# A hybrid decoder trunk on one core: the leftovers of an expert dispatch, the transposes of `hs` and the row additions change places

## The chip, the core and the metric

The kernel runs on one core of one Trainium2 chip as a single program. A core has five instruction queues that work side by side and wait for one another only through semaphores: TensorE (PE; its weight loads are shown apart as PEld), VectorE (DVE), ScalarE (ACT), GpSimd (POOL) and SyncE (SP), which here only issues transfers. The metric is device time in microseconds (us), the median of several runs.

## The reference, cut to what matters

The reference is a decoder trunk of two layers over 256 tokens of width 1024. Each layer mixes tokens (layer 0: an RG-LRU group beside sparse attention; layer 1: a gated short convolution), cross-attends into 256 memory tokens, and then applies a mixture of 16 experts. A final RMS norm closes it. The change touches only the mixture, which both layers run:

```
gate = top-2 experts of the top-1 group, softmax weights        # (256, 16), two nonzeros a row
for e in range(16):
    h = silu(xt @ w_gate[e]) * (xt @ w_up[e])                   # (256, 512)
    y = y + gate[:, e:e+1] * (h @ w_down[e])                    # (256, 1024)
h = h + y
```

## The kernel before, in words

**Dispatch.** Each expert gets at most 64 tokens (`CAP`), so two experts make a pair of 128 rows, and a layer has eight pairs, 0 to 7. `dispatch` builds a 0/1 matrix `Pm` (L561) and multiplies the tokens with it (`gB`, L578, 32 products), which gives the pair's gathered tokens `XgT`, copied out by DVE and ACT in turn (L586, L588). What is left of a dispatch is its inner function `rest`, handed back as `last_part`. For pairs 0 to 5 (`by_rows`) it is two tiny products (`ptC`, L597) and some six small DVE operations (L601 to L608), which give each row its gate weight `gsl` and its destination `row`. For pairs 6 and 7 it transposes `PG`, made on POOL (L564), into `ptC` (L616) and copies that into `PT` (L618, L619).

**A pair.** `expert_pair` is a generator in four pieces, divided by `yield`: the first half of the gate products (`egA`, 16 of the 32 on L714); the second half; the 32 up products (`euA`, also L714) and the activation that makes `hs` (L724 to L726); four transposes of `hs` into `hC` (L731) and the copy `hT` (L733). After those come the 32 down products (`eyA`, `eyO`, L738) and the way back. Pairs 0 to 5 scale the result to `y` and scatter it by an indirect transfer from POOL into the DRAM buffers `yd` (L747). Pairs 6 and 7 split the scaled result into `yh` (ACT, L756) and `yl` (DVE, L757), multiply both with `PT` (`poB`, L761, L762) and add that to the residual `h` on DVE (L215).

**The order.** The loop at the end of `moe` lays the pieces of the next pair between those of the current one: next pair's dispatch, first gate half of the next, transposes of the current, second gate half of the next, down products of the current, up products of the next. Pair 4 (`BREAK`) is the exception: its dispatch stands before a branch for overflowing experts, and the program is divided there into blocks. Inside a block a planner sets every engine's queue when the program is built. It takes, by its own estimates of when inputs, weights and tiles are there, the ready instruction that was written earliest, so that an instruction written later can stand ahead of one that it takes to be waiting. On the chip each queue then keeps that order, ready or not. `first()` raises the priority of what is written inside it. Tiles with the tag `s2` (`Pm`, `PG`, `hs`, `hT`, `yh`, `yl`) share three buffers.

**Rows back.** What the pairs 0 to 5 scattered is read back by `add_rows`, called where the last pair, 7, is dispatched: eight transfers from POOL bring `yd` into two tiles `yr` (L830), and four DVE additions put them on `h` (L833).

**Weights.** SP streams them through a ring of twenty 1 MB places (L672) in the order gate of pair n, down of pair n-1, up of pair n. A place is free once TensorE has used it.

Of the kernel before, what the change touches and what calls it, by code (L numbers as in the profile page):

```python
# [19 lines left out]
D = 1024  # L20
T = 256
TT = 2
# [3 lines left out]
NE = 16  # L26
# [6 lines left out]
BREAK = 4  # L33
# [26 lines left out]
def hybrid_trunk_kernel(ctx: ExitStack, tc: tile.TileContext, x, mem, positions, norm_mix, norm_xattn,  # L60
# [6 lines left out]
    V, S, P, G = nc.vector, nc.scalar, nc.tensor, nc.gpsimd  # L67
# [13 lines left out]
    def bank(tag, name="ps"):  # L81
        return psum[tag].tile([128, 512], F32, tag=tag, name=name + tag)
# [10 lines left out]
    def x8(shape, name, dt=F32):  # L93
        return extra.tile(shape, dt, tag="x", name=name)

    def first(n=4000):
        return tc.high_priority(offset=n)
# [6 lines left out]
    h = const.tile([128, TT, D], F32, name="h")  # L104
# [6 lines left out]
    ident = const.tile([128, 128], F32, name="ident")  # L111
# [100 lines left out]
    def h_add(tt, half, ps, ss=None):  # L212

        hs = h[:, tt, half * 512:(half + 1) * 512]
        V.tensor_add(hs, hs, ps)  # L215
        if ss is not None:
            square_sum(hs, ss[:, half, tt:tt + 1], "S")

    def new_ss():
        ss = sm.tile([128, 2, TT], F32, name="ss2")  # L220
        ss_of_h.append(ss)
        return ss
# [127 lines left out]
    def run(gen, n=10 ** 6):  # L350
        for _ in range(n):
            if next(gen, 0) == 0:
                return
# [290 lines left out]
    def chunks_ahead(l):  # L644

        down = []
        for n in range(NE // 2):
            gate, up, next_down = pair_chunks(l, 2 * n, 4, DOWN_LAST if n == NE // 2 - 1 else DOWN)
            yield from down + gate + up if n == BREAK else gate + down + up
            down = next_down  # L650
        yield from down
# [46 lines left out]
        def used(self, n):  # L698
            pass

    def expert_pair(mp, l, stream, pair, step, cuts, by_rows, ss=None, rest=None):


        XgT = pair[0]
        acc = {}
        for nm in "gu":
            acc[nm] = bank("A", "e" + nm)
            for j0 in range(0, J, step):
                with first() if rest else nullcontext():
                    ws = stream.take(2)  # L710
                    for jj in range(step):
                        j = j0 + jj
                        for i in range(2):
                            P.matmul(acc[nm][i * 64:(i + 1) * 64, :], XgT[:, j, i * 64:(i + 1) * 64], ws[i][jj],  # L714
                                     start=(j == 0), stop=(j == J - 1))
                    stream.used(2)
                    if rest:
                        rest()
                        rest = None
                if nm == "g" and j0 + step in (J // 2, J):  # L720
                    yield
        PT, gsl = pair[1:]
        hs = mp.tile([128, DE], F32, name="hs", tag="s2", bufs=3)
        S.activation(hs, acc["g"], AF.Tanh, scale=0.5)  # L724
        V.scalar_tensor_tensor(hs, hs, 1.0, acc["g"], op0=ALU.add, op1=ALU.mult)  # L725
        V.scalar_tensor_tensor(hs, hs, 0.5, acc["u"], op0=ALU.mult, op1=ALU.mult)  # L726
        yield
        hp = bank("C", "h").rearrange("p (j s) -> p j s", j=4)
        h4 = hs.rearrange("p (f j) -> p f j", j=4)
        for j in range(4):  # L730
            P.transpose(hp[:, j, :], h4[:, :, j], ident)  # L731
        hT = mp.tile([128, 4, 128], F32, name="hT", tag="s2", bufs=3)
        S.copy(hT, hp)  # L733
        yield
        py = [bank("A", "ey"), bank("O", "ey")]

        def down(nh, j, i, w):
            P.matmul(py[nh][i * 64:(i + 1) * 64, :], hT[:, j, i * 64:(i + 1) * 64], w,  # L738
                     start=(j == 0), stop=(j == 3))

        def back_by_rows(nh):
            y = mp.tile([128, 512], F32, name="y", bufs=2)
            if nh:
                V.tensor_scalar(y, py[nh], gsl, None, op0=ALU.mult)
            else:
                S.activation(y, py[nh], AF.Copy, scale=gsl)  # L746
            G.indirect_dma_start(out=Yd[l][nh], out_offset=bass.IndirectOffsetOnAxis(ap=PT[:, 0:1], axis=0), in_=y,  # L747
                                 in_offset=None, bounds_check=2 * T - 1, oob_is_err=False)

        def back(nh):  # L750
            if by_rows:
                return back_by_rows(nh)

            yh, yl = (mp.tile([128, 512], F32R, name=nm, tag="s2", bufs=3) if ss is None else
                      spl.tile([128, 512], F32R, name=nm, tag=t) for nm, t in (("yh", "hi"), ("yl", "lo")))
            S.activation(yh, py[nh], AF.Copy, scale=gsl)  # L756
            V.scalar_tensor_tensor(yl, py[nh], gsl, yh.bitcast(F32), op0=ALU.mult, op1=ALU.subtract)  # L757
            for tt in range(TT):
                po = bank("B", "po")
                ts_ = slice(tt * 128, (tt + 1) * 128)  # L760
                P.matmul(po, PT[:, ts_], yh, start=True, stop=False)  # L761
                P.matmul(po, PT[:, ts_], yl, start=False, stop=True)  # L762
                h_add(tt, nh, po, ss)

        for c0, cn, j0, jn in cuts:
            ws = stream.take(2)
            halves = range(c0 // 512, (c0 + cn) // 512)
            for jj in range(jn):
                for nh in halves:
                    for i in range(2):  # L770
                        down(nh, j0 + jj, i, ws[i][jj][:, nh * 512 - c0:nh * 512 - c0 + 512])
            stream.used(2)
            if j0 + jn == 4:
                for nh in halves:
                    back(nh)

    def moe(l, ring, fill=None, n_fill=0):
        with ExitStack() as mctx:
            mp = mctx.enter_context(tc.tile_pool(name=f"moe{l}", bufs=1, reuse_waits="tile"))
            if fill is not None:  # L780
                run(fill, n_fill)
            stream = Stream(chunks_ahead(l), ring)
# [30 lines left out]
            def overflow():  # L813
                n_over = nc.values_load(over[0:1, 0:1])
                with tc.If(n_over > 0):  # L815
                    with tc.For_i(0, 3, 1):
                        V.tensor_scalar(posm2, posm2, float(-CAP), None, op0=ALU.add)
                        rest = Direct(chunks_in_turn(l), mp)
                        for e in range(0, NE, 2):
                            pairs, last_part = dispatch(mp, l, xs, gate, vals, posm2, e, 2, True, "XgO")  # L820
                            last_part()
                            run(expert_pair(mp, l, rest, pairs[0], 1, DOWN_ROWS, True))

            def add_rows():

                for r in range(2):
                    yr = x8([128, TT, D], "yr")
                    for tt in range(TT):
                        for nh in range(2):
                            nc.gpsimd.dma_start(yr[:, tt, nh * 512:(nh + 1) * 512],  # L830
                                                Yd[l][nh][r * T + tt * 128:r * T + (tt + 1) * 128, :])
                    for tt in range(TT):
                        V.tensor_add(h[:, tt, :], h[:, tt, :], yr[:, tt, :])  # L833

            def experts():

                for n in range(NE // 2):
                    with first() if n == 0 else nullcontext():
                        (pair,), last_part = dispatch(mp, l, xs, gate, vals, posm, 2 * n, 2, n < ROWS_PAIRS)
                        if n:  # L840
                            last_part()
                    last = n == NE // 2 - 1
                    if last:
                        add_rows()
                    yield expert_pair(mp, l, stream, pair, 4, DOWN_LAST if last else DOWN, n < ROWS_PAIRS,
                                      new_ss() if last else None, None if n else last_part)

            pairs = experts()
            cur = next(pairs)
            run(cur, 3)  # L850
            for n in range(1, NE // 2):
                if n == BREAK:
                    nxt = next(pairs)
                    run(cur)
                    overflow()
                    cur = nxt
                    run(cur, 3)
                    continue
                nxt = next(pairs)
                run(nxt, 1)  # L860
                run(cur, 1)
                run(nxt, 1)
                run(cur)
                run(nxt, 1)
                cur = nxt
            run(cur)

# [463 lines left out]
```

## Time and profile before

| what | value |
|---|---|
| runs shown | 972.27 us median of 3 (966.81 to 973.39) |
| the profiled execution | 972.64 us, its span 970.8 us |
| PE, PEld busy | 911.2 us (94%), 592.3 us (61%) |
| DVE, ACT, POOL busy | 395.9, 326.1, 85.2 us |
| mean granted TensorE clock | 0.970 of full speed |
| L714, gate and up products, both layers | 1024 products, 124.0 and 124.9 us busy |
| mixture of layer 0, of layer 1 | from about 278 to 508 us, from about 732 to 962 us of the span |

Times in the rows are microseconds from the start of the span. In a timeline row the first number is the start, the second the duration, `xN` the number of merged instructions, and the bracket the idle time of the engine before the row with what ended it. In the granted clock 1.00 is 2.4 GHz and 0.50 is 1.2 GHz.

### The profile page before, as it was taken

Reading aid. Unit: us, or ns where it says so; the run is one execution under the profiler, and the core shown is the slowest. Engines: PE = TensorE matmul, PEld = TensorE weight load, DVE = VectorE, ACT = ScalarE, POOL = GpSimd, SP = SyncE. Lnnn points to the kernel's source line nnn. Section 1 sums busy time; section 2 is a strip of 40 time slices with the busy share of each in tenths; the row PEclk is TensorE's granted clock in tenths of the full one; section 3 lists DMA queues with packets and bytes.
Section 4 is the critical chain, followed back from the end, with each engine's and each line's share of the span. In section 5 each row is a group of like instructions: output and inputs, shape, how many; then the busy total and the mean of one; then the engine's idle time right before and its main releaser. Section 6 shows DMA issues by size and latency. Waiting matters only on the chain.

```text
span 970.8 us, 13231 instructions
## 1 busy us (share of the span) xinstructions
PE 911.2 (94%) x5197; PEld 592.3 (61%) x5197; DVE 395.9 (41%) x830; ACT 326.1 (34%) x605; POOL 85.2 (9%) x144
## 2 busy tenths in 40 slices
PE   7999999999989997999889999999999999899875
PEld 5898678898754333433338998998875333333321
DVE  6846776645441111111327665644453221111132
ACT  5546575645321111111128444645431111110012
POOL 1000160000020100011100000000011000000201
PEclk9999999999999998999999999999999999999988
DMA  7955166568869999999993555557885999999981
GB/s 256 305 178 115 44 203 189 173 235 322 312 248 422 417 420 413 420 419 420 399 342 118 187 175 179 181 201 294 320 316 233 421 417 421 414 421 417 418 333 43
DMA packets 83023, 285.45 MB, mean 294 GB/s; under 512 B 15112, under 2 KB 16224, under 8 KB 62468
## 3 DMA queue, kind: packets, MB, share of 16 engines
q1 hardware_dynamic: 78468, 272.82, 74.6%
q0 software_dynamic: 4480, 11.65, 3.3%
q8 instruction: 45, 0.74, 0.3%
q14 instruction: 30, 0.25, 0.1%
HBM read 275.94 MB, written 11.53 MB: 296 GB/s over the span
## 4 chain that ended last, share of the span: by engine, by line
PE 34%; issue 14%; DMA 8%; DVE 2%; ACT 1%; POOL 1%; POOLq 0%; ACTq 0%; DVEq 0%
DMA yd<-y,row 5%; PE euA L714 4%; PE FA L316 4%; PE FA L321 4%; PE FA L319 4%; DMA yr<-yd 3%; PE egA L714 3%; PE TA L295 2%; PE TA L296 2%; PE TA L297 2%; PE eyA L738 2%; PE eyO L738 2%; PE gB L578 1%; PE sB L408 1%; PE poB L762 1%
## 5 line engine op out<-in xcount | busy, mean ns | idle before, releaser
L275 DVE TENSOR_TENSOR lo<-w,hi 128x1024 fp32r<-128x1024 f32 x122 | 147.7, 1222 | 124.8 <-ACT hi L274 85.4
L274 ACT CAST hi<-w 128x1024 fp32r<-128x1024 f32 x122 | 125.9, 1047 | 89.0 <-PE FA L321 48.7
L714 PE MATMUL egA<-we,XgT 128*64 128x512 f32 x512 | 124.0, 614 | 8.9 <-DVEq L815 6.4
L714 PE MATMUL euA<-we,XgT 128*64 128x512 f32 x512 | 124.9, 615 | 0.0
L714 PEld LDWEIGHTS egA<-we,XgT 128*64 128x64 f32 x512 | 40.9, 141 | 74.6 <-issue 65.0
L714 PEld LDWEIGHTS euA<-we,XgT 128*64 128x64 f32 x512 | 41.9, 141 | 70.5 <-issue 65.5
L738 PE MATMUL eyA<-we,hT 128*64 128x512 f32 x256 | 70.2, 597 | 3.0 <-ACT hT L733 3.0
L738 PE MATMUL eyO<-we,hT 128*64 128x512 f32 x256 | 72.2, 594 | 0.0
L319 PE MATMUL FA<-xh,hi 128*128 128x256 f32 x272 | 70.4, 292 | 1.9 <-ACT xh L250 1.8
L321 PE MATMUL FA<-xl,hi 128*128 128x256 f32 x272 | 70.0, 290 | 1.8 <-DVE xl L251 1.8
L586 ACT ACTIVATE XgT<-gB,ffn 128x128 f32<-128x128 f32 x64 | 22.5, 367 | 113.8 <-DVE XgT L588 113.8
L319 PEld LDWEIGHTS FA<-xh,hi 128*128 128x128 f32 x272 | 53.2, 196 | 3.8 <-ACT xh L250 2.5
L321 PEld LDWEIGHTS FA<-xl,hi 128*128 128x128 f32 x272 | 53.2, 196 | 3.5 <-DVE xl L251 2.6
L726 DVE SCALAR_TENSOR_TENSOR hs<-hs,euA 128x512 f32<-128x512 f32 x16 | 11.0, 687 | 98.1 <-PE euA L714 98.1
L747 POOL DMA_INDIRECT yd<-y,row x24 | 23.9, 995 | 299.1 <-ACT y L746 226.2
L578 PEld LDWEIGHTS <-xs 128*128 128x128 f16 x512 | 35.3, 148 | 18.4 <-issue 18.4
L738 PEld LDWEIGHTS eyO<-we,hT 128*64 128x64 f32 x256 | 20.9, 137 | 38.1 <-issue 37.0
L725 DVE SCALAR_TENSOR_TENSOR hs<-hs,egA 128x512 f32<-128x512 f32 x16 | 11.0, 687 | 76.2 <-ACT hs L724 76.2
L316 PE MATMUL FA<-xh,lo 128*128 128x256 f32 x272 | 41.9, 285 | 0.0
L578 PE MATMUL gB<-Pm,xs 128*128 128x128 f16 x512 | 38.4, 234 | 2.2 <-DVE Pm L561 2.2
L738 PEld LDWEIGHTS eyA<-we,hT 128*64 128x64 f32 x256 | 19.0, 136 | 34.4 <-issue 29.7
L229 POOL TENSOR_TENSOR rs<-ms,mhalf 128x2 f32<-128x2 f32 x9 | 6.5, 721 | 376.6 <-DVE ms L227 255.3
(419 smaller groups left out, 1547.5 us busy)
## 6 DMA issues: line engine op xcount, KB each, us to landing
we<-in_moe_w_gate_dram SPq DMA_DIRECT2D x58, 1024.0 KB, 13.4
we<-in_moe_w_down_dram SPq DMA_DIRECT2D x54, 1024.0 KB, 14.3
we<-in_moe_w_up_dram SPq DMA_DIRECT2D x52, 1024.0 KB, 18.6
we<-in_moe_w_up_dram SPq DMA_DIRECT2D x24, 512.0 KB, 11.4
w<-in_odd_w_in_dram SPq DMA_DIRECT2D x12, 1024.0 KB, 5.2
w<-in_even_w_in_dram SPq DMA_DIRECT2D x9, 1024.0 KB, 7.9
w<-in_xa_wk_dram SPq DMA_DIRECT2D x8, 1024.0 KB, 6.6
w<-in_xa_wv_dram SPq DMA_DIRECT2D x8, 1024.0 KB, 5.8
```

What stands on the lines that cost most here:

```text
L274: S.copy(hi, t)
L275: V.tensor_sub(lo, t, hi.bitcast(F32))
L295: P.matmul(ps[tt], xh[:, k, sl], hi, start=(k == 0), stop=False)
L296: P.matmul(ps[tt], xh[:, k, sl], lo, start=False, stop=False)
L316: P.matmul(o, lo[:, fs], xh[:, k, :], start=False, stop=(k == J - 1), skip_group_check=True)
L319: P.matmul(o, hi[:, fs], xh[:, k, :], start=(k == 0 and f % 2 == 0), stop=False, skip_group_check=True)
L321: P.matmul(o, hi[:, fs], xl[:, k, :], start=False, stop=False, skip_group_check=True)
L578: P.matmul(ps[:, jj, :], part[:, tt, :, j0 + jj], Pm[:, tt].rearrange("p e s -> p (e s)"), start=(i == 0), stop=(i == 3))
L586: S.activation(Xg[pi][:, j, :], src, AF.Copy, scale=g)
L714: P.matmul(acc[nm][i * 64:(i + 1) * 64, :], XgT[:, j, i * 64:(i + 1) * 64], ws[i][jj], start=(j == 0), stop=(j == J - 1))
L738: P.matmul(py[nh][i * 64:(i + 1) * 64, :], hT[:, j, i * 64:(i + 1) * 64], w, start=(j == 0), stop=(j == 3))
L747: G.indirect_dma_start(out=Yd[l][nh], out_offset=bass.IndirectOffsetOnAxis(ap=PT[:, 0:1], axis=0), in_=y, in_offset=None, bounds_check=2 * ...
```

## The change

Three things change. The call of `last_part` moves from the dispatch into `expert_pair`, behind the first 16 gate products of the same pair, for all pairs but pair 4 (pair 0 had it there before, and keeps `first()` through the new argument `start`). Each of the four transposes of `hs` gets an order-only edge to the TensorE instruction written just before it; for the first transpose that is the last product of the next pair's `last_part`. And `add_rows` is divided: `get_rows` takes both tiles and issues the eight transfers at the dispatch of pair 7, and the four additions are written after pair 7's up products and `hs`, behind the way back of pair 6.

```diff
-    def expert_pair(mp, l, stream, pair, step, cuts, by_rows, ss=None, rest=None):
+    def expert_pair(mp, l, stream, pair, step, cuts, by_rows, ss=None, rest=None, start=False):
...
-                with first() if rest else nullcontext():
+                with first() if rest and start else nullcontext():
...
         for j in range(4):
-            P.transpose(hp[:, j, :], h4[:, :, j], ident)
+
+            tc.keep_in_program_order(P.transpose(hp[:, j, :], h4[:, :, j], ident))
...
-            def add_rows():
-
-                for r in range(2):
-                    yr = x8([128, TT, D], "yr")
+            def get_rows():
+
+                yrs = [x8([128, TT, D], "yr") for _ in range(2)]
+                for r, yr in enumerate(yrs):
                     for tt in range(TT):
                         for nh in range(2):
                             nc.gpsimd.dma_start(yr[:, tt, nh * 512:(nh + 1) * 512],
                                                 Yd[l][nh][r * T + tt * 128:r * T + (tt + 1) * 128, :])
-                    for tt in range(TT):
-                        V.tensor_add(h[:, tt, :], h[:, tt, :], yr[:, tt, :])
+                return yrs
...
                         (pair,), last_part = dispatch(mp, l, xs, gate, vals, posm, 2 * n, 2, n < ROWS_PAIRS)
-                        if n:
-                            last_part()
+                    if n == BREAK:
+                        last_part()
                     last = n == NE // 2 - 1
-                    if last:
-                        add_rows()
                     yield expert_pair(mp, l, stream, pair, 4, DOWN_LAST if last else DOWN, n < ROWS_PAIRS,
-                                      new_ss() if last else None, None if n else last_part)
+                                      new_ss() if last else None, None if n == BREAK else last_part, n == 0)
...
                 nxt = next(pairs)
+                last = n == NE // 2 - 1
+                if last:
+                    yrs = get_rows()
                 run(nxt, 1)
                 run(cur, 1)
                 run(nxt, 1)
                 run(cur)
                 run(nxt, 1)
+                if last:
+                    for yr in yrs:
+                        for tt in range(TT):
+                            V.tensor_add(h[:, tt, :], h[:, tt, :], yr[:, tt, :])
                 cur = nxt
             run(cur)
```

## Rows read from the trace of the kernel before

**Rows 1.** Stretches: PE, PEld, DVE, ACT, POOL busy, granted clock, DMA share, GB/s.
```profile
900.00:925.00 25.00, 22.51 (x109) 8.39 (x110) 3.36 (x5) 2.01 (x4) 7.07 (x12) 1.00 1.01 415
925.00:950.00 25.00, 18.41 (x66) 6.76 (x64) 9.36 (x12) 3.03 (x6) 0.00 (x0) 0.86 0.73 280
```

**Rows 2.** The chain that ended last, end of layer 1's mixture: start, us, what.
```profile
916.74 16.12 DMA yr<-yd
...
932.98 0.11 DVE h L833
...
934.12 0.75 DVE yl L757
```

**Rows 3.** One line, L833: operation, count, ns min/median/max, first and last start.
```profile
L833 DVE TENSOR_TENSOR h<-h,yr x8: 1224/1225/1228, 468.7 to 933.0; 128x1024 f32<-128x1024 f32 x8
```

**Rows 4.** Timeline of PE, layer 1, way back of pair 6, up and down products of pair 7.
```profile
929.09 0.74 PE L761 MATMUL poB<-yh,PT 128*128 128x512 f32 x2
934.92 1.22 PE L762 MATMUL poB<-yl,PT 128*128 128x512 f32 x2 [5.09 <-DVE yl L757]
...
939.97 7.36 PE L714 MATMUL euA<-we,XgT 128*64 128x512 f32 x30
...
949.59 3.65 PE L738 MATMUL eyA<-we,hT 128*64 128x512 f32 x16 [0.73 <-ACT hT L733]
```

**Rows 5.** The same timeline of PE in layer 0.
```profile
479.12 0.73 PE L761 MATMUL poB<-yh,PT 128*128 128x512 f32 x2
481.70 0.73 PE L762 MATMUL poB<-yl,PT 128*128 128x512 f32 x2 [1.85 <-DVE yl L757]
...
485.49 7.62 PE L714 MATMUL euA<-we,XgT 128*64 128x512 f32 x30
```

**Rows 6.** Stretches as in rows 1, the half-speed ones behind these two waits.
```profile
482.00:486.00 4.00, 4.00 (x10) 1.65 (x10) 2.82 (x6) 0.60 (x1) 0.31 (x1) 0.65 1.02 377
...
935.00:940.00 5.00, 5.00 (x10) 1.90 (x10) 2.71 (x4) 0.60 (x1) 0.00 (x0) 0.50 1.03 381
```

**Rows 7.** Timeline of DVE, layer 1, from pair 6's sums to pair 7's `yl`.
```profile
935.75 1.29 DVE L215 TENSOR_TENSOR h<-h,poB 128x512 f32<-128x512 f32 x2
...
940.08 0.42 DVE L618 TENSOR_SCALAR PT<-ptC 128x256 fp32r<-128x256 f32 x1 [0.17 <-PE poB L762]
...
941.01 0.68 DVE L725 SCALAR_TENSOR_TENSOR hs<-hs,egA 128x512 f32<-128x512 f32 x1
...
956.79 0.75 DVE L757 SCALAR_TENSOR_TENSOR yl<-eyA,gsl,yh 128x512 fp32r<-128x512 f32 x1 [8.74 <-PE eyO L738]
```

**Rows 8.** Timeline of PE: `ptC` and `hC` of pairs 5 to 7, up products beside them.
```profile
454.25 0.68 PE L616 MATMUL ptC<-ident,PG 128*128 128x128 f32 x2 [1.65 <-POOL PG L564]
454.86 8.78 PE L714 MATMUL euA<-we,XgT 128*64 128x512 f32 x32
...
906.53 7.09 PE L714 MATMUL euA<-we,XgT 128*64 128x512 f32 x32
914.43 0.75 PE L731 MATMUL hC<-ident,hs 128*128 128x128 f32 x4 [0.82 <-DVE hs L726]
```

**Rows 9.** Timeline of PE, layer 1, `ptC` and `hC` of pairs 2 to 4.
```profile
799.63 0.20 PE L597 MATMUL ptC<-vals,Pm 128*128 128x10 bf16 x2
799.75 3.65 PE L714 MATMUL egA<-we,XgT 128*64 128x512 f32 x16
...
824.92 1.08 PE L738 MATMUL eyA<-we,hT 128*64 128x512 f32 x4 [0.76 <-ACT hT L733]
```

**Rows 10.** Weights of layer 1's pair 7: SP's timeline, landing of L672's, transfers from 925 to 950.
```profile
906.62 0.33 SPq L672 DMA_DIRECT2D we<-in_moe_w_up_dram  x1
...
DMA to landing us min/median/max: 23.5/23.5/23.5
...
GB/s 420 393 416 420 406 410 419 354 420 370 393 380 387 383 387 397 377 383 393 390 380 361 390 374 400 367 361 315 226 98 13 0 0 0 0 0 0 0 0 0
```

**Rows 11.** Timeline of POOL, layer 1, the last seven of the eight transfers that read the rows back.
```profile
913.55 3.72 POOL L830 DMA_DIRECT2D yr<-yd  x7 [1.48 <-DMA yd<-y,row]
```

## The prediction

> **What bounds the kernel now.** I read the stretches first. In the mixture TensorE and the weight stream are both full: 22.51 of 25 us busy at 415 GB/s, and in the next 25 us the stream falls to 280 GB/s while TensorE has 18.41 of 25 us [rows 1]. So the end of a mixture is where TensorE's own idle time costs wall time, since the weights are nearly all there. Then the chain of waits through that end: it goes from the reading back of the scattered rows (16.12 us) over the last row addition to pair 6's `yl` [rows 2]. The reader is to see that `yl` needs none of those rows: it stands behind the additions only because DVE keeps its queue's order. TensorE shows the price: 5.09 us idle in front of `poB` in layer 1 and 1.85 us in layer 0 [rows 4, 5]. Last the clock: behind the two waits it was granted 0.50 in layer 1 (1.2 GHz) and 0.65, a mean of its two levels, in layer 0 [rows 6], after TensorE had been idle; 30 up products took 7.36 and 7.62 us [rows 4, 5] where 32 take 7.09 us at 2.4 GHz [rows 8].
>
> **The additions move.** They and pair 6's four sums (L215) read and write the same `h`, so written behind those sums they can't go ahead of them in DVE's queue, whatever the planner estimates. `yl` then follows `yh` at once. What goes: in layer 1 the stretch from the end of the first `poB` pair, 929.09 + 0.74 = 929.83, to the end of the up products, 939.97 + 7.36 = 947.33, is 17.50 us. In layer 0 it is 479.85 to 493.11, 13.26 us [rows 4, 5]. What must stay in it, by rows: DVE's two `yl` of 0.75 us and two sums of 1.29 us together, 2.8 us, of which 0.7 us lie beside the first `poB` pair, so 2.1 us [rows 2, 7]; another `poB` pair, 0.7 us [rows 4]; and 30 of the 32 up products, 30/32 x 7.09 = 6.65 us [rows 8], as two find room before. With 0.15 us for the signals between them I take 9.6 us for both layers. Bounds: 7.1 us if the way back hides completely beside the up products, and 11.2 us if the stretch still ran at the lower clock for as long as in layer 0 (4 us at 0.65 lose 1.4 us [rows 6]) with 0.2 us of bank waits more. Gain: 17.5 - 9.6 = 7.9 us and 13.26 - 9.6 = 3.7 us, together **11.6 us**; by the bounds 8.4 to 16.6 us.
>
> Where the additions go: four of 1.225 us [rows 3], 4.9 us. Between the sums and pair 7's activation DVE has the 7 us of the up products, with `PT` (0.42 us) and one half of the activation (0.68 us) in them [rows 7]: 6.0 of 7 us, so they hide. If the planner puts them behind the activation, 8.74 us of DVE idle time in front of pair 7's `yl` [rows 7] cover them. Without cover they cost up to 4.9 us a layer; half cover, 2.4 us, is my upper bound. Their rows are in time: the last lands at 916.74 + 16.12 = 932.86 [rows 2], and the first sums would end near 932. The eight transfers stay in the same place of POOL's queue, behind pair 5's scatter, and both tiles were in use at once before too, as seven issues follow each other in 3.72 us [rows 11], ahead of the first addition. SP's queue is not touched. Next late is `hs` of pair 7, and behind it nothing changes: the 970.8 - 947.33 = 23.5 us after it only shift.
>
> **What is left of a dispatch moves.** For pairs 1 to 3 it is two products, 0.20 us, ahead of the gate products, with no idle time around them [rows 9]; behind 16 gate products it costs the same 0.20 us, and its small DVE operations are needed only by the scaling of `y`, a whole down phase later. Zero, at most 0.2 us a pair either way. For pairs 6 and 7 it is `ptC`, for which TensorE waits 1.65 us for POOL, with 32 up products at 8.78 instead of 7.09 us behind it in two of the four cases (the other three waits are like it, 1.65 to 1.67 us) [rows 8]. Would these waits go? The row says no: `ptC` of pair 7 stands ahead of up products of pair 6 that are written earlier. The planner thus sent it out of turn, because it took the up weights to be late. Writing it 16 gate products later doesn't change that, since those gate products wait for weights that come later still. I take zero; both ends are 0 and the 11.6 us of the first rival.
>
> **The transposes are pinned.** The edge goes to one instruction, the last of the next pair's `last_part`, and if that is sent out early the pin holds nothing. In pairs 1 to 3 the transposes already stand behind 16 gate products. Pair 6's, with 0.82 us of wait in each layer [rows 8], would profit from gate products in between; I take zero of 1.6 us for the same reason.
>
> **Sum.** 972.64 us, the profiled execution (0.4 us above the median of the runs shown), less 11.6 us is 961.0 us. Its own range: 972.64 - 16.6 = 956 to 972.64 - 8.4 + 2.4 = 966.6 us, of which 959 to 964 is the likely part.
>
> **First rival: all three edits work.** If `ptC` does stand behind gate products, and pair 6's transposes with it, each layer loses two waits of 1.65 us, one slowed set of up products, 8.78 - 7.09 = 1.69 us, and 0.82 us: 5.8 us, 11.6 us in both [rows 8], which would give 949.4 us. The weights limit that in layer 1: the stream runs dry at about 944.4 us [rows 10], and the last eight of 32 down products, which my forecast has at 949.59 - 7.9 + 1.5 x 3.65 = 947.2 us [rows 4], can't come 5.8 us sooner but 2.8. So 961.0 - 5.8 - 2.8 = 952.4 us. For it: that is where the edits were put in the text. Against it: the queue order of `ptC` in rows 8.
>
> **Second rival: the stream is the bound, and nothing is gained.** At 415 GB/s and a share of 1.01 [rows 1] the transfers can't go faster, so whatever TensorE saves it could give back waiting for weights: 970 to 973 us. The Trainium skill ("Perfetto Trace Analysis", section "Roofline") states about 435 GB/s as the ceiling of a single core's sixteen engines, and by it a stream-bound stage has no room. The 415 GB/s agree with it. Against the rival stand rows: the last up tile of pair 7 was issued at 906.62 and, by the 23.5 us of its kind, lands at 930.1, while 30 of the 32 up products ran from 939.97 on; the last weights are there at about 944.4 [rows 10] and the down products began only at 949.59 [rows 4]. Shifted by 7.9 us they begin at 941.7. If the first down tiles landed as late as 944.4 this would cost 2.7 us of the 11.6.
>
> **Third rival, on the other side: the transposes slip behind the whole gate.** Once pinned, they let the planner send all 32 gate products first; then `hC`, `hT` and the down products stand in a line with nothing between, as at pair 4, where TensorE idles 0.76 us before `eyA` [rows 9]. That is six pairs in each of two layers, 12 x 0.76 = 9.1 us. It alone leaves 970.1 us; where each is followed by a set of products at the lower clock, as the 1.65 us wait was (1.69 us), it is 12 x 2.45 = 29.4 us, and 990 us. It decides from 11.6 / 12 = 0.97 us a place. Against it: the pin's target is written inside the gate's first half, and the 0.76 us wait of rows 9 was followed by down products that took no longer than elsewhere, 1.08 us for four.
>
> **How the numbers follow.** Forecast 0.58, first rival 0.16, second 0.18, third 0.08. About 1% is what a measurement of this kernel can tell from no change, 9.7 us, so the line is at 962.5 us and the forecast lies close to it: some 0.7 of its chance falls below. Faster by over 1%: 0.7 x 0.58 + 0.16 = 0.57. Slower by over 1%: most of the third, 0.06. Within 1%: 0.37. The range from 951 to 969 us holds the first rival, all of the forecast and the partly hidden cases of the second; what it leaves out is most of the second and the third, and more than I count in the first. Likeliest: 961.0 us.
>
> **What would show it.** Right: no idle time of TensorE in front of the second `poB` pair in either layer; L833 in DVE's queue behind L215; the up products of pair 7 in about 7.1 us; `ptC` of pair 7 still ahead of the up products of pair 6 with its 1.65 us. First rival: those waits gone. Second: TensorE waiting for `we`. Third: idle time at `hT` in every pair. I'm wrong if DVE delays pair 7's `hs`, or if the lower clock turns up in stretches that were at full speed.

## The result, and the profile after

The kernel after takes **960.55 us** (median of 4, 958.93 to 963.41), beside 972.83 us for the kernel before on the same chip (median of 4, 966.81 to 973.51): a ratio of 0.989, 95% interval 0.984 to 0.994. The forecast was 961.0 us. In later runs, 24 of before and 11 of after, the difference was 972.49 - 961.86 = 10.63 us, so some of the 12.28 us here is chance. The profiled execution of after has 959.15 us, its span 957.3 us.

TensorE's timeline shows all that the prediction spoke of. The columns are those of [rows 4]; line numbers have moved by one (`poB` L762 and L763, `hC` L732, down products L739).

```profile
453.53 0.68 PE L616 MATMUL ptC<-ident,PG 128*128 128x128 f32 x2 [1.66 <-POOL PG L564]
454.13 7.09 PE L714 MATMUL euA<-we,XgT 128*64 128x512 f32 x32
...
476.70 0.73 PE L762 MATMUL poB<-yh,PT 128*128 128x512 f32 x2
477.49 0.73 PE L763 MATMUL poB<-yl,PT 128*128 128x512 f32 x2
...
480.31 7.08 PE L714 MATMUL euA<-we,XgT 128*64 128x512 f32 x30
...
794.05 3.65 PE L714 MATMUL egA<-we,XgT 128*64 128x512 f32 x16
797.64 0.21 PE L597 MATMUL ptC<-vals,Pm 128*128 128x10 bf16 x2
797.70 0.73 PE L732 MATMUL hC<-ident,hs 128*128 128x128 f32 x4
...
899.99 0.68 PE L616 MATMUL ptC<-ident,PG 128*128 128x128 f32 x2 [1.66 <-POOL PG L564]
900.60 7.09 PE L714 MATMUL euA<-we,XgT 128*64 128x512 f32 x32
908.50 0.75 PE L732 MATMUL hC<-ident,hs 128*128 128x128 f32 x4 [0.81 <-DVE hs L726]
...
923.17 0.73 PE L762 MATMUL poB<-yh,PT 128*128 128x512 f32 x2
923.95 0.73 PE L763 MATMUL poB<-yl,PT 128*128 128x512 f32 x2
924.62 1.07 PE L714 MATMUL euA<-we,XgT 128*64 128x512 f32 x2
925.62 0.50 PE L762 MATMUL poB<-yh,PT 128*128 128x512 f32 x1
...
926.77 7.08 PE L714 MATMUL euA<-we,XgT 128*64 128x512 f32 x30
```

The second `poB` pair now follows the first with no idle time, where [rows 4, 5] have 5.09 and 1.85 us. From the end of the first pair to the end of the up products it is 923.90 to 933.85 = 9.95 us in layer 1 (17.50 before) and 477.43 to 487.39 = 9.96 us in layer 0 (13.26 before): 7.55 + 3.30 = **10.85 us**. But `ptC` of pair 7 still stands ahead of the up products of pair 6 with its 1.66 us, and `hC` of pair 6 still has 0.81 us, as in [rows 8]. Only in pairs 1 to 3 has TensorE's order changed: `ptC` stands behind gate products instead of ahead of them [rows 9].

DVE's timeline of the same end of layer 1, to be held against [rows 7] and the 4.9 us of additions in [rows 3]:

```profile
924.12 0.75 DVE L758 SCALAR_TENSOR_TENSOR yl<-eyO,gsl,yh 128x512 fp32r<-128x512 f32 x1 [0.21 <-ACT yh L757]
924.78 1.27 DVE L215 TENSOR_TENSOR h<-h,poB 128x512 f32<-128x512 f32 x2
...
927.92 0.68 DVE L725 SCALAR_TENSOR_TENSOR hs<-hs,egA 128x512 f32<-128x512 f32 x1
928.52 4.62 DVE L869 TENSOR_TENSOR h<-h,yr 128x1024 f32<-128x1024 f32 x4
933.89 0.69 DVE L726 SCALAR_TENSOR_TENSOR hs<-hs,euA 128x512 f32<-128x512 f32 x1 [0.75 <-PE euA L714]
```

The four additions (L869) run behind the sums and beside the up products, and DVE still idles 0.75 us before it needs pair 7's `euA`. They are hidden, with 0.75 us to spare; layer 0 has the same 0.75 us.

The stretches of [rows 1, 6] again: full clock where it was 0.50 and 0.65, and TensorE has 24.11 of 25 us up to 925 us.

```profile
480.00:484.00 4.00, 4.00 (x20) 1.35 (x20) 4.00 (x6) 0.47 (x2) 0.31 (x1) 1.00 1.03 377
...
900.00:925.00 25.00, 24.11 (x107) 9.04 (x108) 2.32 (x4) 2.24 (x4) 5.63 (x10) 1.00 1.02 412
...
926.00:931.00 5.00, 5.00 (x24) 1.79 (x24) 4.67 (x8) 0.47 (x2) 0.00 (x0) 1.00 1.04 387
```

The chain of waits, in which [rows 2] had the reading back and the last addition, now goes from ScalarE's `yh` to `yl` at once:

```profile
922.43 0.69 ACT yh L757
...
923.15 0.76 DVE yl L758
...
923.95 0.73 PE poB L763 x2
```

**What the rest of the 13.5 us between the two spans is.** In layer 0 the first gate products of pair 4 begin 2.36 us earlier after (382.48 against 384.84); the first ones of the whole mixture begin 2.42 us earlier (278.69 against 281.11), so this lead comes from ahead of the mixture. Pair 4's gate products then run 1.63 us longer, and pair 6's up products take 7.09 instead of 8.78 us, though the same 1.66 us wait is ahead of them. None of this is at a place that the edit changes, and the experiments below have it in other places. So the kernels are compared by one more measure, which leaves out what comes ahead of pair 4: from the first gate product of pair 4 to the end of pair 7's up products, read off each timeline, layer 0 plus layer 1. What it leaves out holds the only pairs in which the moved `ptC` changed TensorE's queue: from the mixture's first gate product to that of pair 4 it is 103.73 and 100.25 us before, 103.79 and 99.76 us after.

| kernel | pair 4 to pair 7's up products, both layers | median | ratio to before, 95% interval |
|---|---|---|---|
| before | 108.27 + 112.85 = 221.1 | 972.5 | 1 |
| after | 104.91 + 105.29 = 210.2 | 960.6 | 0.989 (0.984 to 0.994) |
| after again | 104.95 + 105.27 = 210.2 | 961.9 | 0.990 (0.987 to 0.993) |
| additions only | 105.04 + 105.28 = 210.3 | 962.0 | 0.991 (0.987 to 0.994) |
| dispatch and pins only | 109.92 + 113.20 = 223.1 | 971.4 | 1.000 (0.997 to 1.003) |
| additions of pair 7's tile | 106.24 + 107.88 = 214.1 | 964.7 | 0.994 (0.991 to 0.996) |
| `ptC` pinned, additions back | 108.07 + 109.39 = 217.5 | 966.7 | 0.992 (0.989 to 0.995) |
| `ptC` pinned | 98.44 + 102.07 = 200.5 | 953.4 | 0.982 (0.979 to 0.986) |
| `ptC` pinned, again | 99.27 + 102.39 = 201.7 | 951.5 | 0.980 (0.977 to 0.982) |
| ... and no reading back | 98.49 + 97.68 = 196.2 | 946.7 | 0.974 (0.971 to 0.977) |
| ... rows behind the weights | 98.89 + 97.18 = 196.1 | 953.4 | 0.981 (0.978 to 0.983) |

### The profile page after: what moved, and what is told of

Its sections match the earlier page's. It is cut to its first block, busy times and chain, and to the rows that moved or that the text cites. A ratio compares the mean times of both kernels' runs of the same rounds, so it can differ in the third digit from the quotient of the medians.

```text
span 957.3 us, 13235 instructions
## 1 busy us (share of the span) xinstructions
PE 905.0 (95%) x5197; PEld 588.6 (61%) x5197; DVE 395.6 (41%) x830; ACT 326.0 (34%) x605; POOL 85.7 (9%) x144
## 4 chain that ended last, share of the span: by engine, by line
PE 38%; issue 13%; DMA 5%; DVE 2%; ACT 1%; POOL 0%; POOLq 0%; ACTq 0%
PE euA L714 5%; DMA yd<-y,row 5%; PE egA L714 5%; PE FA L316 4%; PE FA L319 4%; PE FA L321 4%; PE eyA L739 2%; PE TA L296 2%; PE TA L295 2%; PE TA L297 2%; PE eyO L739 2%; PE gB L578 1%; PE sB L408 1%; PE poB L763 1%; DVE yl L758 0%
## 5 line engine op out<-in xcount | busy, mean ns | idle before, releaser
L714 PE MATMUL euA<-we,XgT 128*64 128x512 f32 x512 | 121.4, 602 | 0.0
L739 PE MATMUL eyA<-we,hT 128*64 128x512 f32 x256 | 70.2, 597 | 3.0 <-ACT hT L734 3.0
L739 PE MATMUL eyO<-we,hT 128*64 128x512 f32 x256 | 72.2, 594 | 0.0
L739 PEld LDWEIGHTS eyO<-we,hT 128*64 128x64 f32 x256 | 20.9, 137 | 38.1 <-issue 36.6
L739 PEld LDWEIGHTS eyA<-we,hT 128*64 128x64 f32 x256 | 19.0, 136 | 34.4 <-issue 29.7
```

## The experiments

**The additions alone.** The kernel before with `get_rows` and the additions behind the loop's last piece; `last_part` and the transposes are as before.

```diff
-                    if last:
-                        add_rows()
...
+                if last:
+                    yrs = get_rows()
                 run(nxt, 1)
...
+                if last:
+                    for yr in yrs:
+                        for tt in range(TT):
+                            V.tensor_add(h[:, tt, :], h[:, tt, :], yr[:, tt, :])
```

> The kernel before with one edit alone: the eight transfers stay at the dispatch of pair 7, the four row additions are written behind pair 7's up products. My theory is that these additions are the whole effect: the idle time of TensorE ahead of the second poB pair goes (5.09 us in layer 1, 1.85 us in layer 0), and the time is that of the kernel after, 958 to 963 us, a ratio to before of about 0.989. The rival, that what is left of a dispatch and the pinned transposes each carry a share, expects a time between the two, 964 to 970 us.

Measured: 961.95 us, ratio 0.991, and both stretches around pair 7's up products are 9.96 us. This edit is the whole effect: TensorE's, ScalarE's and POOL's queues are those of the kernel before, and in DVE's only the additions have moved.

**The other two edits alone.** The kernel after with the additions put back.

```diff
-                last = n == NE // 2 - 1
-                if last:
-                    yrs = get_rows()
+                if n == NE // 2 - 1:
+                    add_rows()
...
-                if last:
-                    for yr in yrs:
-                        for tt in range(TT):
-                            V.tensor_add(h[:, tt, :], h[:, tt, :], yr[:, tt, :])
```

> The kernel after with the row additions put back where they were, so that only the moved last_part and the pinned transposes are left. My theory: no change, 970 to 974 us, with 5 us of idle time ahead of the second poB pair of layer 1 as before; in pairs 1 to 3 two small products (0.20 us) stand behind 16 gate products instead of ahead of them. The rival, that these two edits bring a share, expects 961 to 969 us; that the pins cost something, over 975 us.

Measured: 971.35 us, ratio 1.000 (0.997 to 1.003). TensorE's timeline has the old wait, 3.72 us in layer 1, shown here, and 3.25 in layer 0 (I had expected 5 in layer 1; pair 6's up products took 8.78 instead of 7.09 us in this run, so TensorE came later to the wait):

```profile
935.83 1.22 PE L763 MATMUL poB<-yl,PT 128*128 128x512 f32 x2 [3.72 <-DVE yl L758]
...
940.89 7.46 PE L714 MATMUL euA<-we,XgT 128*64 128x512 f32 x30
```

and DVE's shows the last addition, held by its rows, right ahead of `yl`:

```profile
933.89 1.23 DVE L834 TENSOR_TENSOR h<-h,yr 128x1024 f32<-128x1024 f32 x1 [2.52 <-DMA yr<-yd]
935.03 0.75 DVE L758 SCALAR_TENSOR_TENSOR yl<-eyA,gsl,yh 128x512 fp32r<-128x512 f32 x1
```

The queues of the kernels before and after, compared instruction by instruction, say why: in the blocks of pairs 4 to 7 TensorE's queue is the same. It differs in `ptC` of pairs 1 to 3 alone, DVE's queue in one `XgT` copy of each of those pairs and in the additions.

**After again.**

> The kernel after once more beside the others, on the same chip: 958 to 963 us. It shows how far one profile's stretches at the lower granted clock differ from another's of the same kernel: of the 13.5 us between the two spans, 10.85 us lie in the two stretches around pair 7's up products, and the rest in stretches at 0.50 that the edit does not touch. If that rest belongs to the edit, the same stretches are at full speed again here; if it is chance, they come in other places.

Measured: 961.86 us, ratio 0.990; the stretches are 9.96 and 9.95 us. Pair 6's up products in layer 0, 7.09 us in the first profile of this kernel, are at the lower clock here, as they were before:

```profile
457.56 0.68 PE L616 MATMUL ptC<-ident,PG 128*128 128x128 f32 x2 [1.66 <-POOL PG L564]
458.17 8.78 PE L714 MATMUL euA<-we,XgT 128*64 128x512 f32 x32
```

So that 1.7 us belonged to one run and not to the edit; pair 4 began at 388.17 us in this run.

**`ptC` pinned.** What the moved `last_part` needs to stay where it is written.

```diff
-                    P.transpose(ptp[:, tt * 128:(tt + 1) * 128],
-                                PG[:, tt, 2 * pi:2 * pi + 2, :].rearrange("p e s -> p (e s)"), ident)
+                    tc.keep_in_program_order(
+                        P.transpose(ptp[:, tt * 128:(tt + 1) * 128],
+                                    PG[:, tt, 2 * pi:2 * pi + 2, :].rearrange("p e s -> p (e s)"), ident))
```

> The kernel after, and the two transposes of PG into ptC for pairs 6 and 7 also get the order-only edge to the instruction written just before them, the last of 16 gate products of their pair. My theory of why two of the three edits brought nothing is that ptC was sent ahead of up products that are written earlier, so that the pin on hS's transposes held nothing. With ptC held, hC stands behind 16 gate products too: four waits of 1.65 us and two of 0.81 us go, and one set of up products at the lower clock (1.7 us), 4.1 us in layer 0 and 5.8 us in layer 1, where the weights leave 4.4 us (the stream ends at about 937.2 us and the last eight down products begin at about 941.6 us). That is 8.5 us less than the kernel after, about 952 us. The rival, that the weight stream is the bound by now, expects 957 to 961 us, the waits turning up again in front of we.

Measured: 953.43 us, 8.4 us less than after on the same chip; its interval ends at 0.986, that of after begins at 0.987. In the second set of runs it had 951.52 us. It beats both kernels. TensorE's timeline in layer 1:

```profile
899.50 3.61 PE L715 MATMUL egA<-we,XgT 128*64 128x512 f32 x16
903.04 0.44 PE L617 MATMUL ptC<-ident,PG 128*128 128x128 f32 x2
903.32 0.65 PE L733 MATMUL hC<-ident,hs 128*128 128x128 f32 x4
903.89 3.65 PE L715 MATMUL egA<-we,XgT 128*64 128x512 f32 x16
...
913.81 1.08 PE L740 MATMUL eyA<-we,hT 128*64 128x512 f32 x4 [1.12 <-DMA we<-in_moe_w_down_dram]
...
926.34 3.65 PE L715 MATMUL euA<-we,XgT 128*64 128x512 f32 x14 [1.36 <-DMA we<-in_moe_w_up_dram]
```

`ptC` and `hC` stand between the two halves of the gate products without a wait. What is late next are the weights: three waits for `we`, 1.12, 0.20 and 1.36 us, so layer 1 gains only 105.27 - 102.07 = 3.2 us where layer 0 gains 6.5. I had expected 4.4 and 4.1: the sum came out right, its parts didn't. The pin also changes more than these places: in TensorE's queue six up products in each layer, and four down products in layer 1, have moved too, so the gain isn't shown to be the waits alone.

**`ptC` pinned, the additions back in their old place** (both edits above together).

> The kernel with ptC pinned, but with the row additions back where they were before. It asks whether the two gains simply add. If they do, 971.4 - 8.4 = 963 us. My theory is that they do not: TensorE comes sooner to the way back of pair 6, but the rows that the additions wait for come with the weight stream and the end of pair 5, which is only some 1.7 us sooner, so yl waits longer; I expect 966 to 970 us, with idle time ahead of the second poB pair of 6 to 9 us in layer 1.

Measured: 966.70 us. The waits that the pin removes come back in front of `yl`:

```profile
478.94 1.22 PE L764 MATMUL poB<-yl,PT 128*128 128x512 f32 x2 [8.35 <-DVE yl L759]
...
929.87 1.22 PE L764 MATMUL poB<-yl,PT 128*128 128x512 f32 x2 [6.61 <-DVE yl L759]
```

By the table the pin is worth 223.1 - 217.5 = 5.6 us with the additions in the old place and 210.2 - 200.5 = 9.7 us with them moved. The gains don't add, because the rows don't keep up. Measured from pair 4's first gate product, TensorE ends its first `poB` pair 8.3 and 6.8 us sooner than without the pin (layers 0 and 1), but the last addition, which waits for its rows, starts only 3.2 and 3.9 us sooner.

**Additions of a ready tile**, first try: is it the additions' time on DVE or the wait for their rows?

```diff
-                        V.tensor_add(h[:, tt, :], h[:, tt, :], yr[:, tt, :])
+                        V.tensor_add(h[:, tt, :], h[:, tt, :], xsh[:, tt, :])
```

> The kernel before, with the four additions where they were, but they add a tile that has been in place since the start of the mixture (the high half of xs) instead of the rows read back; the eight transfers still run. So the sum lacks the rows. It tells the additions' wait for their rows from their own work on DVE. My theory: the whole price is the wait for the last of the rows, so the idle time ahead of the second poB pair goes in both layers and the time is 960 to 964 us. The rival, that 4.9 us of additions ahead of yl are the price, expects most of the kernel before, 968 to 973 us.

Measured: 977.19 us, slower than before (ratio 1.005, 1.003 to 1.007), which neither theory expected. The row of line L833 says where the additions went:

```profile
L833 DVE TENSOR_TENSOR h<-h,xs x8: 1210/1262/1785, 273.3 to 739.0; 128x1024 f32<-128x1024 f32 x8
```

Needing nothing late, they were sent to the start of each mixture, where the routing waits for DVE. The time tells nothing about their old place, though the stretches are 9.96 and 9.95 us here too, and from pair 4 to pair 7's up products it is 107.64 + 107.11 = 214.8 us: what is lost lies ahead of that. The second try adds a tile that is made right ahead of them:

```diff
-                        V.tensor_add(h[:, tt, :], h[:, tt, :], yr[:, tt, :])
+                        V.tensor_add(h[:, tt, :], h[:, tt, :], X7.rearrange("p j s -> p (j s)"))
...
-                        add_rows()
+                        add_rows(pair[0])
```

`X7` is the tile `XgT` of pair 7.

> The second try at the question of the ready tile. In the first try the four additions needed nothing late and ran at the start of the mixture (273.3 and 739.0 us), where DVE holds up the routing, so the time said nothing about their place. Here they add XgT of pair 7, written right ahead of them by DVE, so they stay in the old place of the queue and are ready some 20 us ahead of the rows; the transfers still run, and the sum lacks the rows. My theory: the price was the wait for the rows, so both stretches are 9.96 us and the time is 960 to 964 us. The rival, that 4.9 us of additions in that place are the price, expects 968 to 973 us.

Measured: 964.74 us, ratio 0.994, a little over my 964 and under the rival's 968. Both stretches are 9.96 us. But this try didn't keep the old place either: in DVE's queue the additions stand ahead of pair 5's `y` here, and behind it and behind pair 6's `hs` in the kernel before. The question is settled by the trace of before, where DVE idles 5.83, 4.11, 2.94 and 2.04 us ahead of the four additions of layer 1, each time for rows. The last one:

```profile
932.98 1.22 DVE L833 TENSOR_TENSOR h<-h,yr 128x1024 f32<-128x1024 f32 x1 [2.04 <-DMA yr<-yd]
```

With the additions gone from there, DVE idles 14.70 us ahead of pair 6's first `yl` (kernel after), room enough for 4.9 us of additions that need not wait. So the wait for the rows was the price. The 214.1 - 210.2 = 3.9 us left over are a cost of the new place. POOL's timeline:

```profile
901.78 1.86 POOL L564 TENSOR_TENSOR PG<-Pm,gate 128x128 f32<-128x128 f16 x2
```

TensorE's:

```profile
902.35 0.33 PE L616 MATMUL ptC<-ident,PG 128*128 128x128 f32 x1 [1.83 <-POOL PG L564]
903.69 0.48 PE L616 MATMUL ptC<-ident,PG 128*128 128x128 f32 x1 [1.01 <-POOL PG L564]
```

and DVE's, with the additions at the same time:

```profile
898.54 4.84 DVE L833 TENSOR_TENSOR h<-h,XgT 128x1024 f32<-128x1024 f32 x4 [0.43 <-ACT XgT L586]
```

`PG` takes 1.86 instead of 0.76 us beside them, and `ptC` waits 2.84 instead of 1.66 us, in both layers; behind it pair 6's up products of layer 1 took 8.36 instead of 7.09 us.

**Additions twice**, to find the edge of their new cover.

```diff
-                    for yr in yrs:
+                    for yr in yrs + yrs:
```

> The kernel after with the four row additions done twice (eight in place of four; the rows are counted twice). It measures how much cover the additions have in their new place. The trace of after leaves DVE idle for 0.75 us behind them, and pair 7's hs waits behind them in the queue. My theory: 4.62 more us of DVE, 0.75 of them covered, make hs 3.9 us later in each layer, 7.7 us in both and 969.6 us; up to 974 us if the lower clock follows the wait as it did before. The rival, that the 8.75 us of idle time ahead of pair 7's yl or other idle time covers them as well, expects 961 to 964 us.

Measured: 975.87 us, ratio 1.003: more than either theory. DVE's timeline and TensorE's in layer 1:

```profile
939.87 9.17 DVE L869 TENSOR_TENSOR h<-h,yr 128x1024 f32<-128x1024 f32 x8
```

```profile
949.69 1.13 PE L732 MATMUL hC<-ident,hs 128*128 128x128 f32 x4 [4.49 <-DVE hs L726]
951.54 5.45 PE L739 MATMUL eyA<-we,hT 128*64 128x512 f32 x16 [0.73 <-ACT hT L734]
```

The wait grew by 4.49 - 0.78 = 3.71 us, near the 3.9 expected. But from the end of the up products to pair 7's first `poB` it is 13.52 us (945.20 to 958.72) beside 7.64 after, 5.9 us more, and 6.1 us more in layer 0: the 16 down products behind the wait took 5.45 and 5.68 us instead of 3.65, at the granted 0.50. The lower clock adds 2.2 to 2.4 us a layer to a wait of 3.7 us.

**No reading back**, with `ptC` pinned: what holds the end of layer 1 then?

```diff
-                    yrs = get_rows()
+                    yrs = []
```

> The kernel with ptC pinned, without the eight transfers that read the rows back and without the four additions (the rows are missing from the sum). It asks what holds the end of layer 1 once ptC is pinned: there TensorE waits 1.12, 0.20 and 1.36 us for we. My theory: the transfers themselves; 2 MB fewer, some 4.9 us of the stream at 420 GB/s, let the last weights land earlier, and these 2.7 us go: 950 to 951 us. The rival, that the weights are late because their places in the ring come free late or because SP is held up issuing them, expects the waits to stay and 953 to 954 us.

Measured: 946.67 us. The waits for `we` are gone, and layer 1 is 102.07 - 97.68 = 4.4 us shorter. Stretches, columns as in [rows 1]: first without the transfers, then with them (`ptC` pinned). The last window of each is partly empty: 82 of 379 GB/s fill 1.1 us of it, 97 of 383 GB/s fill 1.3 us. So the stream ends at about 926.1 and 936.3 us, which is 103.0 and 108.4 us after pair 4's first gate product (823.07 and 827.92 us).

```profile
920.00:925.00 5.00, 3.49 (x16) 1.33 (x16) 0.69 (x1) 0.58 (x1) 0.00 (x0) 1.00 1.01 379
925.00:930.00 5.00, 4.99 (x22) 1.52 (x20) 0.00 (x0) 0.69 (x1) 0.00 (x0) 1.00 0.21 82
```

```profile
930.00:935.00 5.00, 3.51 (x18) 1.60 (x20) 0.69 (x1) 0.58 (x1) 0.00 (x0) 1.00 1.03 383
935.00:940.00 5.00, 4.99 (x22) 1.36 (x18) 0.55 (x1) 0.69 (x1) 0.00 (x0) 1.00 0.24 97
```

So the transfers themselves made the weights late. I had counted only the 2.7 us of waits that the timeline shows. Of the rest 1.5 us lie in pair 6's down products: four of them stand elsewhere in TensorE's queue here, and from the first of the 32 to the first `poB` product it is 7.46 instead of 10.06 us, of which 1.12 were a wait. This part isn't shown to be the stream's.

**The rows behind the weights**, an attempt to win these 4.4 us with the rows still read.

```diff
-                if last:
-                    yrs = get_rows()
+                if last and l == 0:
+                    yrs = get_rows(nc.gpsimd)
...
+                if last and l:
+                    yrs = get_rows(nc.sync)
```

> The kernel with ptC pinned, and in layer 1 the eight transfers that read the rows back are issued from SP's queue behind the last weights instead of from POOL at the dispatch of pair 7. Leaving these transfers out took 4.4 us off layer 1, since the weights then land sooner; here they still run, but last. Expected: the waits for we go, the stream of weights ends at about 931 instead of 936 us and the rows land by about 936 us, in the idle time of DVE ahead of pair 7's sums; the sums wait for them 1 to 2.5 us, so 2 to 3.4 us less than with ptC pinned alone: 950 to 951.5 us. The rival: the rows land so late that the last sums wait for them longer, 953 us and more.

Measured: 953.36 us, no better than with `ptC` pinned alone (951.52 us on the same chip). The rival's time came, but not for its reason: the rows weren't late. SP's timeline and the landing of its transfers:

```profile
924.96 5.61 SPq L832 DMA_DIRECT2D yr<-yd  x8
...
yr<-yd SPq DMA_DIRECT2D x8, 256.0 KB, 5.3
```

The last one was issued at 930.2 us and landed at about 935.5, ahead of the first addition at 937.33. From pair 4 to pair 7's up products layer 1 is as short as without the transfers (97.18 us, against 102.39 with `ptC` pinned again), but these 5.2 us are given back: from there to the last `poB` product it is 20.8 instead of 14.3 us. DVE's timeline, then TensorE's:

```profile
936.66 0.75 DVE L759 SCALAR_TENSOR_TENSOR yl<-eyO,gsl,yh 128x512 fp32r<-128x512 f32 x1 [2.54 <-DMA gf<-in_norm_final_dram]
937.33 3.49 DVE L872 TENSOR_TENSOR h<-h,yr 128x1024 f32<-128x1024 f32 x3
```

```profile
941.68 0.77 PE L763 MATMUL poB<-yh,PT 128*128 128x512 f32 x1 [5.78 <-DVE h L215]
```

DVE idled 2.54 us ahead of the second `yl`, and the additions stand behind it in the queue. There they hold up the sums and, through them, the last `poB` products by 5.78 us: the fault of the kernel before with the places exchanged.

## Why the prediction was right

**The additions: right in mechanism and place, 0.75 us off in size.** I took 9.6 us for both stretches and 11.6 us of gain; they are 9.95 and 9.96 and the gain 10.85 us, in every profile that has this edit and no wait for weights there. The mis-sized term is "30 of the 32 up products, 30/32 x 7.09 = 6.65 us". The 30 take 7.08 us, as long as 32 do, and the two that found room take 1.07 us, as four do elsewhere (1.08 us). The two gain nothing; that a 64-column product left without its neighbour costs as much as both together is my reading of these rows and wasn't tried by itself. The other terms came out right only in sum, which is luck. I had DVE's `yl` and sums (2.1 us), a `poB` pair (0.7) and signals (0.15), 2.95 us. In the rows of after TensorE has no idle time there, so DVE's work and the signals cost nothing: what stands there is the second `poB` pair up to 924.62, the two up products up to 925.62 and four single `poB` products up to 926.77, 0.72 + 1.00 + 1.15 = 2.87 us.

**The additions' new cover: right.** The rows land 1.4 us ahead of the first addition (last issued at 910.74, 16.4 us), and 0.75 us of DVE are left. The bound for partly hidden additions was too low: it counted DVE's own time, and the additions done twice show that TensorE's wait brings 2.2 to 2.4 us of lower clock with it.

**`last_part`: zero, right**, and the step that it rests on holds: `ptC` of pairs 6 and 7 was sent ahead of products that are written earlier, and with the call moved TensorE's queue is still the same there. That the planner did so because it took the up weights to be late wasn't looked at. **The pins: zero, right**: their target was sent ahead, too.

**First rival: it fell, but its price came out right, in part by luck.** Its sum for the edits really working was 952.4 us. One more pin makes them work, and the time is 951.5 to 953.4 us. Its limit, 2.8 us for layer 1, stands beside 3.2 and 2.9 us measured (105.27 less 102.07 and 102.39), but it had the weights late at pair 7's last down products, which don't wait for them; the waits came at pair 6's down and pair 7's up products. In layer 0 it had 5.8 us. The profile has 6.5, although pair 4's gate products ran 1.6 us longer in it (10.04 against 8.43 us), so some 2.3 us have another source, which wasn't separated.

**Second rival: it fell for this change** and begins to come true one edit later: after has no such wait for `we`, with `ptC` pinned there are three. The Trainium skill ("Perfetto Trace Analysis", section "Roofline") puts a single core's sixteen DMA engines at about 435 GB/s. The trace agrees: with `ptC` pinned layer 1 had 383 to 426 GB/s at a share of 1.00 to 1.04 in each 5 us from 880 to 935 us.

**Third rival: fell.** The idle time in front of `eyA` is at pair 4 (0.76 us) and at pair 7 (0.73 us, [rows 4]) alone, both as before. In pairs 1 to 3 `hC` still stands between the two halves of the gate.

## What to carry to other kernels

A wait in a chain can belong to the queue and not to the data: where an instruction needs nothing of the one in front of it, ask whether that one can be written behind the first work that it does share data with. Where a planner sets the queues, moving a line in the text may move nothing; read the order of the queue after the edit, and pin the instruction that was sent out of turn and not the one behind it. Before a second saving is added to a first, look whether both end at the same transfer, as the late rows and the weights did here.

## What the runs showed of the hardware

**A wait of TensorE in front of `poB` cost more than its length.** The stretch around pair 7's up products in six cases of late `yl` (both layers of before, of the other two edits alone, and of `ptC` pinned with the additions back), beyond the 9.95 or 9.96 us of the kernel after: 1.85 us of wait cost 3.30, 3.25 cost 4.71, 3.72 cost 6.29, 5.09 cost 7.55, 6.61 cost 9.25 and 8.35 cost 11.17 us. So 1.5 us were added to the two short ones and 2.5 to 2.8 us to the four long ones. The granted clock behind them was 0.50: in layer 1 of before from 935 to 939 us, of the other two edits from 936 to 940, of the pinned kernel from 930 to 934 and in its layer 0 from 479 to 484; behind the two short ones only for about 2 us (484 to 486, 485 to 487). The amount isn't fixed for other waits: behind the 1.65 us in front of `ptC` the up products were slowed in two of four places before, and in one and in two of four in the two profiles of after. The prediction had the sizes for two of these only.

**POOL's `PG` beside DVE's additions** took 0.52 and 1.37 us instead of 0.41 and 0.40. The Trainium skill ("SBUF — State Buffer", section "Who interferes with whom") says that a DVE instruction with two SBUF inputs contends with a GpSimd instruction that reads SBUF, and calls the ports that they share an exclusive lock. The trace agrees: both inputs of the additions lie in SBUF, the slower `PG` (902.27 to 903.64) ends 0.26 us behind the addition beside it (901.96 to 903.38), and its 0.97 us more are under the 1.22 us of one addition.
